# Two-layer hybrid mixer step: the 1/rms table through memory, spatial weights loaded earlier, new tokens' scores after the attention

## The chip, the cores and the metric

The kernel runs on one core of one Trainium2 chip. The metric is the device time of one launch in microseconds; before the change it is 2384.72 us, the median of three runs (2384.2 to 2386.24).

## The reference

One inference step of a two-layer decoder on 1,024 prompt tokens (width 1,024) and 8 new tokens, each with its own cache. A layer computes `h = RMSNorm(x)`, one wide projection `h @ w_in`, four branches of width 384, and a gated merge:

```
h = rms_norm(x, norm_g)
A: y = a_b * conv3(a_c * a_h)                   # short causal convolution
B: window attention, distances 0..128, 6 heads, sinks, rotary
C: y = c_u * (tril(w_spatial) @ LN(c_v) + b_spatial)   # chunks of 128 positions
D: three head pairs, windows (128,1), (512,4), (2048,16), rotary,
   weighted by their softmax denominators
out = x + (sum_n sigmoid(h @ w_merge)_n * ((y_n * silu(gate_n)) @ w_branch_n)) @ w_out
```

The new tokens run through the same layer; their attention reads keys and values of the caches instead of the prompt's. Outputs are both token groups after a final norm, and the updated caches.

## The kernel before, in words

All activations are kept channel by partition, 1,032 columns wide: 8 new tokens, then 1,024 prompt tokens. A float32 product is made of three matmuls on a high and a low half of each operand (L178, L181, L182; L372, L375, L376 for the groups whose tokens lie on the partitions). `hh` and `hl` hold the halves of `x * g` without the factor 1/rms; that factor is applied behind the products. Token-major results take it from `rtok` (one column of 128 tokens per block), channel-major ones from `rr`, a table with all 1,032 factors in every partition, and the rotation takes it through `cosT` and `sinT`, which are multiplied by `rr` once per layer.

Each weight tile is loaded by SP into `wr`, rounded by ACT into `wh` (L154), and its rest made by POOL into `wl` (L156). Weight tiles have few buffers, so the projections run in the order of the program.

Per layer the order of the program is: projections of window keys and the first window queries (`rope_products`); 1/rms (L324 to L338); the first value group `tm_v` (L408) with 9 blocks of 8 x 3 matmuls, one block of tokens after another; more window queries; the chunk branch's values `tm_group` with their statistics; the second value group; the spatial branch (L441 to L484); window attention `attend` (L632); gates; and three dilated groups, `branch_d(0..2)`. For each dilated group the new tokens' scores `decD.scores` (L651 to L668) come before the group's attention, `attention()`. They transpose the queries (L656), write them to memory and read them back into every partition (L659, L661), multiply them by the cached keys on POOL (L662), sum on DVE (L663), and take the new token's own key in a small matmul (L667). After the third group come a projection, `decode_finish` (L680 to L719: softmax over the cached keys on 8 partitions, transposed back at L713), then the weights of the three groups (`al` to `at`, L919 to L945, with the transpose at L934), the loads of the chunk branch's result `y` from memory (L952), the values of the new tokens (`values`, L731 and L733, put between the chunks of the last two gate projections), and the merge (L1000 to L1011), whose first operand `yh`, `yl` is made from `y` (L979, L980).

1/rms, before: the mean square per token is taken to `rtok`, then 9 diagonal matrices `dg` are made on DVE (L332), and a matmul with a matrix of ones (L333) puts each block's factors into all partitions.

Tiles carry a tag; the tiles of one tag share a fixed number of buffers: `ms` (small PSUM results) and `acc` (projections) three each, `dec` (caches, values, spatial weights, `y`) three, `slot` 34. Within a tag a new tile takes a buffer that an earlier one has given back.

The program's order is not the order on the engines: the framework plans all five engines with simulated times and issues what is ready by its plan, with the program's order as priority. Each engine then runs its own list in order. Inside `attend` a few groups of matmuls are pinned to the program's order (L531). `load(dst, src, dist)` ties an SP load to the projection that is `dist` marks back, and so sets how far ahead it may be issued.

Of the kernel before, what the change touches and what calls it, by code (L numbers as in the profile page):

```python
# [7 lines left out]
F32 = mybir.dt.float32  # L8
F32R = mybir.dt.float32r
AF = mybir.ActivationFunctionType  # L10
ALU = mybir.AluOpType
AX = mybir.AxisListType

P = 128
# [3 lines left out]
NS = 8  # L18
T = SEQ + NS
CH = 344  # L20
NCH = 3
MIX = 384
# [10 lines left out]
def kernel(ctx: ExitStack, tc: tile.TileContext, i, o, c):  # L33
    nc = tc.nc
    pe, act, dve, pool, sp = nc.tensor, nc.scalar, nc.vector, nc.gpsimd, nc.sync
# [5 lines left out]
    sm = ctx.enter_context(tc.tile_pool(name="sm", bufs=1))  # L41
# [13 lines left out]
    def dec(shape, name):  # L55
        return sl.tile(shape, F32, tag="dec", name=name, bufs=3)
# [7 lines left out]
    def pmisc():  # L64
        return psM.tile([P, 512], F32, tag="ms", name="ms")
# [4 lines left out]
    def dscr(name, shape):  # L70
        return dr.tile(shape, F32, tag=name, name=name)
# [20 lines left out]
    def load(dst, src, dist):  # L92
        d_ = sp.dma_start(dst, src)
        if len(marks) >= dist:
            tc.add_manual_dep(d_.ins, marks[-dist].name, nosync, reason="prefetch distance")


    ident = cp.tile([P, P], F32, name="ident")
# [3 lines left out]
    onesm = cp.tile([P, P], F32, name="onesm")  # L102
# [21 lines left out]
    for l in range(2):  # L124
# [5 lines left out]
        for b in range(NS):  # L130
# [5 lines left out]
            n = 2047 * 256 // 8  # L136
# [30 lines left out]
    def w_pair(l, c0, j):  # L167
        r = split_w([P, KT, P], [
            (lambda t: t[:, :, 0:64], win_cols(l, c0 + 64 * j, 64)),
            (lambda t: t[:, :, 64:128], win_cols(l, c0 + 192 + 64 * j, 64))])  # L170
        copy_piece()
        return r
# [78 lines left out]
    for n0, n1 in GROUPS:  # L251
        off = NS if n0 == 0 else 0
        cs = slice(NS + n0 * P - off, NS + n1 * P)
        w = cs.stop - cs.start
        for k in range(KT):
            ks_ = slice(k * P, (k + 1) * P)
            ps = pmisc() if k % 2 else pacc()
# [12 lines left out]
    for n in range(9):  # L270
        src, M = (xin[n], P) if n < 8 else (xs, NS)
        act.activation(junk[:M, :DM], src[:M, :DM], AF.Square, accum_out=sq0[:M, n:n + 1])

    for l in range(2):
# [31 lines left out]
        def rope_tile(w, name):  # L306
            return rope(rope_products([w], [slot(name)])[0])
# [5 lines left out]
        cosT, sinT = slot("cosT"), slot("sinT")  # L313
        load(cosT, c["cos"], 2)
        load(sinT, c["sin"], 2)
        rr, rtok = slot("rr"), sm.tile([P, 9], F32, tag="rtok", name="rtok", bufs=2)
        if l == 0:
            pt_ = sq0
        else:
            pt_ = pmisc()  # L320
            for n in range(9):
                cols, M = (blkcols(n), P) if n < 8 else (slice(0, NS), NS)
                pe.matmul(pt_[:M, n:n + 1], ssq[:, cols], onesm[:, 0:1], start=True, stop=True)
        for ps_, M in ((slice(0, 8), P), (slice(8, 9), NS)):  # L324
            act.activation(rtok[:M, ps_], pt_[:M, ps_], AF.Sqrt, bias=epst[:M], scale=1.0 / DM)
            dve.reciprocal(rtok[:M, ps_], rtok[:M, ps_])
        for n0, n1 in ((8, 9), (0, 4), (4, 8)):
            ps = pmisc()
            M = NS if n0 == 8 else P
            for n in range(n0, n1):  # L330
                dg = sm.tile([P, P], F32, tag="dg", name="dg", bufs=2)
                dve.tensor_scalar(dg[:M, :M], ident[:M, :M], rtok[:M, n:n + 1], None, op0=ALU.mult)  # L332
                pe.matmul(ps[:, (n - n0) * P:(n - n0) * P + M], onesm[:M], dg[:M, :M], start=True, stop=True)  # L333
            cs = slice(0, NS) if n0 == 8 else slice(NS + n0 * P, NS + n1 * P)
            w = cs.stop - cs.start
            act.activation(rr[:, cs], ps[:, :w], AF.Copy)
            dve.tensor_tensor(cosT[:, cs], cosT[:, cs], rr[:, cs], op=ALU.mult)
            pool.tensor_tensor(sinT[:, cs], sinT[:, cs], rr[:, cs], op=ALU.mult)  # L338
        cw = sm.tile([P, 3, 3], F32, tag="cw", name="cw")
        for t in range(3):  # L340
            load(cw[:, :, t], i["conv_w"][l, t].rearrange("(j p) -> p j", p=P), 2)
# [5 lines left out]
        bview = i["b_spatial"][l].rearrange("(j h) t -> h j t", h=2)  # L347
# [35 lines left out]
        def tm_v(srcs, off):  # L383

            vn = [sl.tile([P, 4, 256], F32, tag="slot", name=f"vn{off}{q}") for q in range(2)]

            def vdst(n):
                return vn[n // 4][:, n % 4] if n < 8 else vsam[:, off:off + 256]

            def ev(n, M, ps):  # L390
                act.activation(vdst(n), ps, AF.Identity, scale=rtok[:M, n:n + 1])
                if n < 8:
                    act.dma_start(vscr[n * P:(n + 1) * P, off:off + 256], vdst(n))
            tm_group(srcs, 4, ev)
            for nm, c0 in (("swa_p", 0), ("dil_p0", 128), ("dil_p1", 256), ("dil_p2", 384)):
                c1 = c0 - off
                if c1 not in (0, P):
                    continue
                dst = o[nm][l, 0, :, 1].rearrange("t h d -> t (h d)")
                nb = dst.shape[0] // P  # L400
                for n in range(nb):
                    act.dma_start(dst[n * P:(n + 1) * P, :], vdst(8 - nb + n)[:, c1:c1 + P])
                dst = o[nm.replace("_p", "_s")]
                dst = dst[l, :, dst.shape[2] - 1, 1].rearrange("b h d -> b (h d)")
                act.dma_start(dst, vsam[:, c0:c0 + P])

        kB, qB = rope(kq[0]), [rope(kq[1])]
        tm_v([(S_V, P), (D_V, P)], 0)  # L408
        qB.append(rope_tile(w_pair(l, S_Q, 1), "qB1"))
        cvt = [sl.tile([P, 2, MIX], F32, tag="slot", name=f"cv{q}") for q in range(4)]  # L410
        lnst = sm.tile([P, 9, 6], F32, tag="lnst", name="lnst")
# [26 lines left out]
            return t  # L438


        lngb, wsps = dec([P, T], "lngb"), dec([P, T], "wsp")  # L441
        wsp = wsps[:, 0:6 * P].rearrange("p (g s) -> p g s", g=6)
        bsps = [lngb[:, 6 * P:7 * P], lngb[:, 7 * P:8 * P], wsps[:, 6 * P:7 * P]]
        for h in range(2):
            for j in range(3):
                load(bsps[j][h * 64:(h + 1) * 64], bview[h, j].partition_broadcast(64), 2)
        load(lngb[:, 0:MIX], i["v_ln_g"][l].partition_broadcast(P), 2)
        load(lngb[:, MIX:2 * MIX], i["v_ln_b"][l].partition_broadcast(P), 2)
        for n in range(9):
            M = P if n < 8 else NS  # L450
            if n == 0:
# [5 lines left out]
            dve.tensor_tensor(v, v, lngb[:M, 0:MIX], op=ALU.mult)  # L457
            dve.tensor_tensor(v, v, lngb[:M, MIX:2 * MIX], op=ALU.add)
        store_later(2, o["chunk_v_s"][l].rearrange("b s c -> (b s) c"), cvs)
        load(wsp, i["w_spatial"][l].rearrange("g t s -> t g s"), 2)  # L460
        wsT = dec([P, 6, P], "wsT")
        for g0 in (0, 3):
            ps = pmisc()
# [6 lines left out]
        for j in range(3):  # L470
            ps = pmisc()
            pe.transpose(ps[:, :NS], cvs[:, j * P:(j + 1) * P], ident[:NS, :NS])
            dve.tensor_scalar(yC[j][:, 0:NS], ps[:, :NS], ws0[:, j:j + 1], bsps[j][:, 0:1], op0=ALU.mult, op1=ALU.add)
            for n0 in (0, 4):
                ps = pmisc()
                for n in range(4):
                    for h in range(2):
                        g = 2 * j + h
# [120 lines left out]
        for j in range(4):  # L599
            t = sm.tile([P, NS], F32, tag=f"qbs{j}", name=f"qbs{j}")  # L600
# [286 lines left out]
        decD = Decode("D")  # L887
        rows, attention = branch_d(0, ends)
        conv_a(0, rows)
        decD.scores(0, dqs[0], dks[0])  # L890
        attention()
        conv_a(1)
        in_a(0)
        decB = Decode("B")
# [8 lines left out]
        rows, attention = branch_d(1)  # L903
        in_a(1)
        rows()
        decD.scores(1, dqs[1], dks[1])
        attention()
        out_a(1)
        conv_a(2)
        rows, attention = branch_d(2)  # L910
        sg0 = gate_d(0)
        rows()
        decD.scores(2, dqs[2], dks[2])
        attention()
        in_a(2)
        values_d = decD.finish(OD)

# [15 lines left out]
        ps = pmisc()  # L933
# [39 lines left out]
        for bi, n in enumerate(order):  # L973
            yh, yl = [], []
            yy = ynext
            for j in range(3):
                t = yy[j]
# [5 lines left out]
            for m in range(KT):  # L983
# [14 lines left out]
                for ch in range(NCH):  # L998
                    cs = slice(ch * CH, (ch + 1) * CH)
# [4 lines left out]
                    t = ctmp("th")  # L1004
# [66 lines left out]
        for m in range(KT - NTAIL):  # L1071
            w = wout(m)
# [4 lines left out]
        for n0, n1 in GROUPS:  # L1077
            c0 = NS + n0 * P if n0 else 0
            cs = slice(c0, NS + n1 * P)
# [66 lines left out]
```

## Time and profile before

| | |
|---|---|
| median of three runs | 2384.72 us |
| the profiled execution | 2387.34 us, span 2385.6 us |
| TensorE (PE) busy | 2365.5 us, 99%; weight loads (PEld) 97% |
| DVE, POOL, ACT busy | 38%, 35%, 29% |
| chain that ended last | PE 98% |
| matmuls of L178, L181, L182 | 27% of the chain each |
| granted TensorE clock, mean | 0.991 |
| DMA | 235.82 MB, mean 99 GB/s |

A page describes one profiled execution. Busy time is the time in which an engine had an instruction running; a wait is put down to what ended last before the waiting instruction began. The clock is the share of full speed that TensorE was granted in a stretch. In the timelines `PE` is a matmul, `PEld` its weight load, `SPq` and `ACTq` the issuing of DMAs; the bracket at the end of a row is the idle time of the engine before it, and what ended it.

### The profile page before, as it was taken

Reading aid. Unit: us, or ns where it says so; the run is one execution under the profiler, and the core shown is the slowest. Engines: PE = TensorE matmul, PEld = TensorE weight load, DVE = VectorE, ACT = ScalarE, POOL = GpSimd, SP = SyncE. Lnnn points to the kernel's source line nnn. Section 1 sums busy time; section 2 is a strip of 40 time slices with the busy share of each in tenths; the row PEclk is TensorE's granted clock in tenths of the full one; section 3 lists DMA queues with packets and bytes.
Section 4 is the critical chain, followed back from the end, with each engine's and each line's share of the span. In section 5 each row is a group of like instructions: output and inputs, shape, how many; then the busy total and the mean of one; then the engine's idle time right before and its main releaser. Section 6 shows DMA issues by size and latency. Waiting matters only on the chain.

```text
span 2385.6 us, 38754 instructions
## 1 busy us (share of the span) xinstructions
PE 2365.5 (99%) x15896; PEld 2305.1 (97%) x15896; DVE 895.2 (38%) x1938; ACT 687.4 (29%) x1522; POOL 843.5 (35%) x556
## 2 busy tenths in 40 slices
PE   7999999999999999999999999999999999999999
PEld 6999999999999999999999999999999999999999
DVE  4345466335312222324333455554452221213143
ACT  5133432223212222223322244323231221212243
POOL 3333234432223444434442322353322233444330
PEclk9999999999899999999999999999989999999999
DMA  7342423433322212224542423244442122222232
GB/s 237 98 123 79 119 69 109 132 102 106 100 71 88 77 55 97 64 70 123 150 146 72 145 72 98 69 151 113 111 126 67 58 91 66 98 67 62 75 99 101
DMA packets 295962, 235.82 MB, mean 99 GB/s; under 512 B 52756, under 2 KB 279696, under 8 KB 293416
## 3 DMA queue, kind: packets, MB, share of 16 engines
q1 hardware_dynamic: 267952, 206.25, 28.8%
q10 hardware_dynamic: 27832, 27.10, 4.1%
q8 instruction: 124, 2.03, 0.4%
q14 instruction: 54, 0.44, 0.1%
HBM read 192.35 MB, written 76.47 MB: 113 GB/s over the span
## 4 chain that ended last, share of the span: by engine, by line
PE 98%; DVE 1%; DMA 0%; ACT 0%; SPq 0%; issue 0%; ACTq 0%; DVEq 0%
PE acc L181 27%; PE acc L182 27%; PE acc L178 27%; PE acc L372 2%; PE acc L375 2%; PE acc L376 2%; PE sc L540 2%; PE ms L569 2%; PE ms L558 1%; PE ms L733 1%; PE ms L479 0%; PE ms L1042 0%; DMA wr<-in_w_in_dram 0%; DVE xT L264 0%; DVE h0l L209 0%; PE ms L333 0%
## 5 line engine op out<-in xcount | busy, mean ns | idle before, releaser
L156 POOL TENSOR_TENSOR wl<-wr,wh 128x384 fp32r<-128x384 f32 (+2 forms) x228 | 476.9, 2093 | 827.3 <-ACT wh L154 698.7
L181 PE MATMUL acc<-h1l,wh 128*128 128x344 f32 x1584 | 511.5, 323 | 0.0
L182 PE MATMUL acc<-h0h,wl 128*128 128x344 f32 x1584 | 510.4, 323 | 0.0
L178 PE MATMUL acc<-h0h,wh 128*128 128x344 f32 x1584 | 509.3, 322 | 0.9 <-DVE xT L264 0.9
L178 PE MATMUL acc<-h1h,wh 128*128 128x344 f32 x1584 | 510.2, 322 | 0.0
L182 PE MATMUL acc<-h1h,wl 128*128 128x344 f32 x1584 | 509.5, 322 | 0.0
L181 PE MATMUL acc<-h0l,wh 128*128 128x344 f32 x1584 | 508.9, 321 | 0.0
L154 ACT ACTIVATE wh<-wr 128x384 fp32r<-128x384 f32 (+2 forms) x228 | 205.2, 901 | 421.4 <-PE acc L181 393.6
L1005 DVE TENSOR_TENSOR th<-acc,rr 128x344 f32<-128x344 f32 x192 | 99.1, 516 | 553.5 <-PE acc L182 553.5
L181 PEld LDWEIGHTS acc<-h1l,wh 128*128 128x128 f32 x1584 | 299.9, 189 | 4.2 <-issue 3.6
L181 PEld LDWEIGHTS acc<-h0l,wh 128*128 128x128 f32 x1584 | 299.2, 189 | 3.9 <-issue 3.5
L182 PEld LDWEIGHTS acc<-h1h,wl 128*128 128x128 f32 x1584 | 299.7, 189 | 2.8 <-issue 2.3
L178 PEld LDWEIGHTS acc<-h0h,wh 128*128 128x128 f32 x1584 | 299.1, 189 | 2.8 <-issue 1.2
L182 PEld LDWEIGHTS acc<-h0h,wl 128*128 128x128 f32 x1584 | 298.6, 189 | 2.9 <-issue 2.3
L178 PEld LDWEIGHTS acc<-h1h,wh 128*128 128x128 f32 x1584 | 299.6, 189 | 1.4 <-issue 1.0
L1011 POOL TENSOR_TENSOR mg<-mg,th 128x344 f32<-128x344 f32 x144 | 134.0, 931 | 303.3 <-DVE th L1010 303.3
L1006 ACT ACTIVATE th<-th 128x344 f32<-128x344 f32 x192 | 94.3, 491 | 496.9 <-DVE th L1005 496.4
L178 PE MATMUL acc<-yh,wh 128*128 128x344 f32 x576 | 184.4, 321 | 0.0
L182 PE MATMUL acc<-yh,wl 128*128 128x344 f32 x576 | 184.3, 320 | 0.0
L181 PE MATMUL acc<-yl,wh 128*128 128x344 f32 x576 | 184.1, 320 | 0.0
L181 PE MATMUL acc<-ml,wh 128*128 128x344 f32 (+3 forms) x384 | 123.2, 321 | 0.0
L182 PE MATMUL acc<-mh,wl 128*128 128x344 f32 (+3 forms) x384 | 123.0, 321 | 0.0
(278 smaller groups left out, 3256.6 us busy)
## 6 DMA issues: line engine op xcount, KB each, us to landing
wr<-in_w_merge_dram SPq DMA_DIRECT2D x64, 512.0 KB
out_dram<-in_cache_dil_kv_dram SPq DMA_DIRECT2D x128, 255.9 KB
wr<-in_w_in_dram SPq DMA_DIRECT2D x60, 512.0 KB
y<-yscr SPq DMA_DIRECT2D x18, 516.0 KB
wr<-in_w_branch_dram SPq DMA_DIRECT2D x48, 192.0 KB
wr<-in_w_in_dram SPq DMA_DIRECT2D x32, 256.0 KB
wr<-in_w_out_dram SPq DMA_DIRECT2D x16, 512.0 KB
out_dram<-in_cache_dil_kv_dram SPq DMA_DIRECT2D x16, 511.0 KB
```

Of the source, the lines that this page charges most:

```text
L154: act.activation(hi, raw, AF.Copy)
L156: pool.tensor_tensor(lo, raw, hi.bitcast(F32), op=ALU.subtract)
L178: mm = pe.matmul(ps[:, :n], hi[:, k], xh[k][:, cs], start=(k == 0), stop=False)
L181: pe.matmul(ps[:, :n], hi[:, k], xl[k][:, cs], start=False, stop=False)
L182: pe.matmul(ps[:, :n], lo[:, k], xh[k][:, cs], start=False, stop=(k == kt - 1))
L372: mm = pe.matmul(ps[:M, :N], lh, hi[:, k % kk], start=(k == 0), stop=False)
L375: pe.matmul(ps[:M, :N], ll, hi[:, k % kk], start=False, stop=False)
L376: pe.matmul(ps[:M, :N], lh, lo[:, k % kk], start=False, stop=(k == KT - 1))
L540: pin(pe.matmul(ps[:, h, a * 256:a * 256 + u.nk], u.qs[h], u.ks[h], start=True, stop=True))
L1005: dve.tensor_tensor(t, pg[:, :CH], rr[:, cs], op=ALU.mult)
L1006: act.activation(t, t, AF.Tanh, scale=0.5)
L1011: pool.tensor_tensor(mg[m][:, cs], mg[m][:, cs], t, op=ALU.add)
```

## The change

Three edits. 1/rms: `rtok` is written to a scratch in memory by two ACT stores, in token order, and read back by one SP load that repeats it in all 128 partitions; `cosT` and `sinT` are multiplied over their full width. Spatial weights: the loads of `lngb`, `bsps` and `wsp` move from behind the second value group to behind the first, ahead of the second window query projection. New tokens' scores: in all three dilated groups `decD.scores` moves behind `attention()`.

```diff
--- before.py
+++ after.py
@@ -324,18 +324,13 @@
         for ps_, M in ((slice(0, 8), P), (slice(8, 9), NS)):
             act.activation(rtok[:M, ps_], pt_[:M, ps_], AF.Sqrt, bias=epst[:M], scale=1.0 / DM)
             dve.reciprocal(rtok[:M, ps_], rtok[:M, ps_])
-        for n0, n1 in ((8, 9), (0, 4), (4, 8)):
-            ps = pmisc()
-            M = NS if n0 == 8 else P
-            for n in range(n0, n1):
-                dg = sm.tile([P, P], F32, tag="dg", name="dg", bufs=2)
-                dve.tensor_scalar(dg[:M, :M], ident[:M, :M], rtok[:M, n:n + 1], None, op0=ALU.mult)
-                pe.matmul(ps[:, (n - n0) * P:(n - n0) * P + M], onesm[:M], dg[:M, :M], start=True, stop=True)
-            cs = slice(0, NS) if n0 == 8 else slice(NS + n0 * P, NS + n1 * P)
-            w = cs.stop - cs.start
-            act.activation(rr[:, cs], ps[:, :w], AF.Copy)
-            dve.tensor_tensor(cosT[:, cs], cosT[:, cs], rr[:, cs], op=ALU.mult)
-            pool.tensor_tensor(sinT[:, cs], sinT[:, cs], rr[:, cs], op=ALU.mult)
+
+        rscr = dscr(f"rscr{l}", [T])
+        act.dma_start(rscr[0:NS], rtok[:NS, 8])
+        act.dma_start(rscr[NS:T].rearrange("(n i) -> i n", i=P), rtok[:, 0:8])
+        sp.dma_start(rr, rscr.partition_broadcast(P))
+        dve.tensor_tensor(cosT, cosT, rr, op=ALU.mult)
+        pool.tensor_tensor(sinT, sinT, rr, op=ALU.mult)
         cw = sm.tile([P, 3, 3], F32, tag="cw", name="cw")
         for t in range(3):
             load(cw[:, :, t], i["conv_w"][l, t].rearrange("(j p) -> p j", p=P), 2)
@@ -406,6 +401,15 @@
 
         kB, qB = rope(kq[0]), [rope(kq[1])]
         tm_v([(S_V, P), (D_V, P)], 0)
+        lngb, wsps = dec([P, T], "lngb"), dec([P, T], "wsp")
+        wsp = wsps[:, 0:6 * P].rearrange("p (g s) -> p g s", g=6)
+        bsps = [lngb[:, 6 * P:7 * P], lngb[:, 7 * P:8 * P], wsps[:, 6 * P:7 * P]]
+        for h in range(2):
+            for j in range(3):
+                load(bsps[j][h * 64:(h + 1) * 64], bview[h, j].partition_broadcast(64), 2)
+        load(lngb[:, 0:MIX], i["v_ln_g"][l].partition_broadcast(P), 2)
+        load(lngb[:, MIX:2 * MIX], i["v_ln_b"][l].partition_broadcast(P), 2)
+        load(wsp, i["w_spatial"][l].rearrange("g t s -> t g s"), 2)
         qB.append(rope_tile(w_pair(l, S_Q, 1), "qB1"))
         cvt = [sl.tile([P, 2, MIX], F32, tag="slot", name=f"cv{q}") for q in range(4)]
         lnst = sm.tile([P, 9, 6], F32, tag="lnst", name="lnst")
@@ -438,14 +442,6 @@
             return t
 
 
-        lngb, wsps = dec([P, T], "lngb"), dec([P, T], "wsp")
-        wsp = wsps[:, 0:6 * P].rearrange("p (g s) -> p g s", g=6)
-        bsps = [lngb[:, 6 * P:7 * P], lngb[:, 7 * P:8 * P], wsps[:, 6 * P:7 * P]]
-        for h in range(2):
-            for j in range(3):
-                load(bsps[j][h * 64:(h + 1) * 64], bview[h, j].partition_broadcast(64), 2)
-        load(lngb[:, 0:MIX], i["v_ln_g"][l].partition_broadcast(P), 2)
-        load(lngb[:, MIX:2 * MIX], i["v_ln_b"][l].partition_broadcast(P), 2)
         for n in range(9):
             M = P if n < 8 else NS
             if n == 0:
@@ -457,7 +453,6 @@
             dve.tensor_tensor(v, v, lngb[:M, 0:MIX], op=ALU.mult)
             dve.tensor_tensor(v, v, lngb[:M, MIX:2 * MIX], op=ALU.add)
         store_later(2, o["chunk_v_s"][l].rearrange("b s c -> (b s) c"), cvs)
-        load(wsp, i["w_spatial"][l].rearrange("g t s -> t g s"), 2)
         wsT = dec([P, 6, P], "wsT")
         for g0 in (0, 3):
             ps = pmisc()
@@ -887,8 +882,8 @@
         decD = Decode("D")
         rows, attention = branch_d(0, ends)
         conv_a(0, rows)
+        attention()
         decD.scores(0, dqs[0], dks[0])
-        attention()
         conv_a(1)
         in_a(0)
         decB = Decode("B")
@@ -903,15 +898,15 @@
         rows, attention = branch_d(1)
         in_a(1)
         rows()
+        attention()
         decD.scores(1, dqs[1], dks[1])
-        attention()
         out_a(1)
         conv_a(2)
         rows, attention = branch_d(2)
         sg0 = gate_d(0)
         rows()
+        attention()
         decD.scores(2, dqs[2], dks[2])
-        attention()
         in_a(2)
         values_d = decD.finish(OD)
```

## Rows read from the trace of the kernel before

**Rows 1.** Part 1 of the page: engine, busy us, share of the span, instructions.

```profile
PE 2365.5 (99%) x15896; PEld 2305.1 (97%) x15896; DVE 895.2 (38%) x1938; ACT 687.4 (29%) x1522; POOL 843.5 (35%) x556
```

**Rows 2.** Waits of TensorE: line, releaser, us in total, times, longest.

```profile
PE ms L333 <- DVE dg L332: 3.8, 3, 1.5
```

**Rows 3.** Timeline of TensorE, layer 0, first value group: start us, us, line, tiles, form.

```profile
50.42 0.28 PE L372 MATMUL acc<-wh,h0h 128*128 128x256 f32 x1
...
71.77 0.28 PE L372 MATMUL acc<-wh,h0h 128*128 128x256 f32 x1
...
79.92 0.28 PE L372 MATMUL acc<-wh,h0h 128*8 128x256 f32 x1
...
82.67 0.32 PE L178 MATMUL acc<-h0h,wh 128*128 128x344 f32 x1
```

**Rows 4.** Windows: stretch, length, busy us of PE, PEld, DVE, ACT, POOL, clock, DMA.

```profile
52.10:55.60 3.50, 0.66 (x5) 0.49 (x4) 3.49 (x4) 0.62 (x3) 3.34 (x3) 1.00 0.25 60
55.60:60.30 4.70, 4.70 (x28) 4.70 (x28) 0.57 (x2) 0.00 (x0) 0.00 (x0) 0.64 0.99 263
```

**Rows 5.** Timeline of TensorE, layer 1, first value group.

```profile
1222.38 0.38 PE L372 MATMUL acc<-wh,h1h 128*128 128x256 f32 x1
...
1251.61 0.32 PE L178 MATMUL acc<-h1h,wh 128*128 128x344 f32 x1
```

**Rows 6.** Tile `wl`, 38 to 62 us: ns min/median/max, first and last start.

```profile
L156 POOL TENSOR_TENSOR wl<-wr,wh x3: 1798/2364/2417, 41.1 to 53.4; 128x1024 fp32r<-128x1024 f32 x2, 128x768 fp32r<-128x768 f32 x1
```

**Rows 7.** Timeline of SP and of ACT, first 12 us.

```profile
2.15 0.41 SPq L242 DMA_DIRECT2D gcol<-in_norm_g_dram  x1
...
6.32 1.28 ACT L207 ACT_TABLE_LOAD   x1 [6.32 <-DMA gcol<-in_norm_g_dram]
```

**Rows 8.** Chain that ended last: start us, us, line, count.

```profile
131.87 0.65 PE sc L540 x8
```

**Rows 9.** Timeline of DVE, layer 0, spatial branch.

```profile
159.85 3.84 DVE L457 TENSOR_TENSOR cv<-cv,lngb 128x384 f32<-128x384 f32 x8 [3.44 <-DMA lngb<-in_v_ln_g_dram]
```

**Rows 10.** Timeline of TensorE, layer 0, third dilated attention and its end.

```profile
542.98 0.27 PE L656 MATMUL ms<-ident,dqs 128*8 128x128 f32 x1
...
579.79 0.66 PE L569 MATMUL ms<-pt,v 128*64 128x128 f32 x8
580.38 0.82 PE L680 MATMUL ms<-ident,sd 128*8 128x128 f32 x6
...
592.64 0.53 PE L713 MATMUL ms<-ident,sx 8*128 8x8 f32 x6
593.10 0.29 PE L934 MATMUL ms<-ident,ew 128*48 128x128 f32 x1
...
596.88 1.09 PE L733 MATMUL ms<-pd,cD 128*64 128x1 f32 x16
```

**Rows 11.** Timeline of DVE, same stretch.

```profile
554.54 1.22 DVE L663 TENSOR_REDUCE sd<-qb 128x16 f32<-128x1024 f32 x1 [5.38 <-POOL qb L662]
...
582.34 0.21 DVE L932 TENSOR_TENSOR ew<-ew,mx 128x48 f32<-128x48 f32 x1
...
589.27 0.95 DVE L709 TENSOR_TENSOR sx<-sx,dw 8x774 f32<-8x774 f32 x1
...
613.54 3.03 DVE L980 TENSOR_TENSOR yl<-y,yh 128x1032 fp32r<-128x1032 f32 x1 [0.60 <-ACT yh L979]
```

**Rows 12.** Timeline of SP's queue, same stretch.

```profile
595.17 4.04 SPq L944 DMA_DIRECT2D at<-ascr  x6
...
607.42 0.32 SPq L93 DMA_DIRECT2D y<-yscr  x1
```

**Rows 13.** Windows, end of the third dilated attention, both layers.

```profile
580.40:616.60 36.20, 36.20 (x258) 35.30 (x257) 23.88 (x45) 8.89 (x15) 8.18 (x4) 0.81 0.54 138
1751.50:1787.00 35.50, 35.50 (x254) 34.60 (x253) 23.06 (x44) 8.79 (x15) 8.97 (x4) 0.81 0.56 142
```

**Rows 14.** Timeline of POOL, layer 0, window branch's gate.

```profile
422.66 3.88 POOL L748 TENSOR_TENSOR OB<-OB,th 128x344 f32<-128x344 f32 x4 [7.02 <-DVE OB L736]
```

## The prediction

> **What bounds the kernel now.** The first thing to read is part 1 of the page: TensorE is busy for 99% of the span, every other engine for less than 40% [rows 1]. So another engine's work or a DMA counts only where it leaves TensorE idle, slows its clock or adds instructions to it. The list of waits of TensorE shows how little is left to win: the one wait that the change touches is that of L333 for `dg`, 3.8 us over both layers [rows 2]. The next view is the timeline of TensorE at the two places where its stream is disturbed, and the windows around them with the granted clock; these are the start of each layer, where the edit to 1/rms stands, and the end of the third dilated attention, where the moved scores stand.
>
> The profiled execution took 2387.34 us around its span of 2385.6; the median of the runs shown is 2384.72. I work out a difference against the profiled execution and apply it to the median.
>
> **Part 1, 1/rms through memory: what goes.** Each layer loses 9 small matmuls (18 instructions of L333), 9 DVE products `dg`, three ACT copies and their waits. The worth is read from the value group that they cut into, from its first matmul to the first matmul behind it. In layer 0 that is 50.42 to 82.67, 32.25 us [rows 3]. Undisturbed, such matmuls start every (79.92 - 71.77) / 69 = 0.118 us (69 of them start between those two rows), and the group has 9 blocks x 8 x 3 = 216, so 25.5 us. The disturbance costs 6.7 us. It includes an idle stretch of 2.84 us (52.10 to 55.60, 0.66 busy) and 4.7 us at a granted clock of 0.64 behind it, which is (1 - 0.64) x 4.7 = 1.7 us [rows 4]. In layer 1 the group takes 1251.61 - 1222.38 = 29.23 us [rows 5], so the disturbance costs 3.7 us. The most that can be won is 10.4 us.
>
> What is late next in layer 0 is the second half of the group's weights: `wl` of that half is not ready before about 53.4, when POOL begins its next one [rows 6]. TensorE stopped at 52.1, so 1.3 us of the idle stretch stay; whether the clock falls for them as it did for 2.84 us is open (0 to 1.7 us). Bounds 10.4 - 1.3 - 1.7 = 7.4 and 10.4; I take 8.5, nearer the lower end because the weights are a row and not a guess.
>
> **Part 1: what comes.** Two small ACT stores with 1,032 four-byte elements, one SP load that waits for them and copies 4 KB to 128 partitions, one DVE and one POOL product of 1,032 columns instead of three of each. No row has that store. The nearest is the load of `gcol`, 2,048 four-byte elements: issued at 2.15, and ACT stood until 6.32 for it, 4.2 us [rows 7]. The broadcast is of the shape of `qb`, whose round trip is in the 12.8 us below. TensorE's wait for `dg`, which needs the same 1/rms, begins at 52.1, so the table is in SBUF by about 52 + 4.2 + 12.8 = 69 at the latest, and its first user on TensorE, the first scores, runs at 131.87 [rows 8]. Hidden, 0; if all of the cover were gone it would be those 17 us. Behind the load on SP stand weight loads that are issued far ahead; behind the products on DVE and POOL stands only the rotation that needs them.
>
> **Part 2, spatial weights earlier.** Nine loads, none new, move ahead of two projection groups. What waits today is DVE, 3.44 us for `lngb` [rows 9]; TensorE has no row of waiting for them. The window attention can begin sooner since its value tile takes a buffer that the spatial work holds, but a stage whose TensorE is full gains nothing from an earlier start. I take 0; bounds -1 and +1, SP's extra issues against DVE's wait.
>
> **Part 3, new tokens' scores behind the attention.** This is the part that can cost. The PSUM tiles `ms` have three buffers, and the trace shows them handed out in program order: `sd` is complete at 555.76 (L663), but its transposes (L680) start at 580.38, right behind the last result matmul (L569, 579.79); `ew` is ready at 582.55 (L932), but its transpose (L934) starts at 593.10, right behind L713 [rows 10, 11]. So in the changed program the transpose of the query (L656), today at 542.98 and inside the attention, starts where L680 starts now. From L656 to the end of L663 is 555.76 - 542.98 = 12.8 us, a round trip through two DMAs, POOL and DVE; L680 moves back by that. From L680 to L713 are 12.3 us now; 2.4 of them are TensorE coming late (L709 ends at 590.22) and some 1.4 are the `al` chain ahead on DVE, both of which the longer wait absorbs: about 8.5 are left. L713 comes at 580.4 + 12.8 + 8.5 = 601.7 instead of 592.64, 9 us later; I take off 0.5 for an attention without the scores in its way.
>
> Does the merge wait for that? L934 (in order behind L713) feeds `ewt`, `ascr`, the `at` loads and, on the same SP queue behind them, the loads of `y` [rows 12]; the last of these also needs the buffer that the last value matmul frees. The split of the last `y` (L980) ends at 616.57 [rows 11], and the merge cannot go past its first product before. From the attention's end to there is 36.2 us, and the windows show TensorE full all along, at a clock of 0.81 (0.81 in layer 1 too) [rows 13]: 36.2 x 0.81 = 29.3 us of work at full clock. So there is nothing in hand: work and chain end together today, and a chain that is 8.5 us longer is idle time, less what the last `y` catches up. Bounds per layer 3 and 12.8; I take 7, two layers 14. The other two moved scores are not on such a chain; those of the first group delay the window branch's, where POOL already stands 7.02 us [rows 14] without any idle time of TensorE, so 0, at worst 3.
>
> What the clock adds is the last question. The rows show it falling behind idle time (0.64) and also inside the full stretch above, whose one-column value matmuls are slow. The Trainium skill, "TensorE: Matmul & The Clock Gate" (Part 1, on the clock gate), says that the gate follows how busy the array has been, and that idle gaps between bursts put it back to half rate. By that rule each new gap before the merge costs another 1.7 us as in [rows 4], and the sum would be 3.4 us higher. The rows agree behind the 2.84 us gap.
>
> **Sum.** -8.5 + 0 + 14 = +5.5 us: 2390.2 for the median, 2392.8 for a profiled execution like the one shown.
>
> **Rivals.** *Covered* (faster): the scores of the third group find a place earlier, or gate tiles fill TensorE until the merge, and each layer loses 1 us or less. It decides at whether L656 runs before the last L569. For it: POOL, DVE and SP have room during the attention. Against it: the order rows above. -8.5 + 2 = -6.5, 2378. *Half covered*: the chain's shift is 4 us, since plan and execution already differ by the 2.4 us seen at L713; -8.5 + 7 = -1.5, 2383. *Chain in full*: 12.8 us per layer, DVE standing for `qb` while gate products wait behind it as it stood 5.38 us at L663; -7.4 + 25.6 = +18, 2403. *The stall stays*: the idle time at 52 was the weights' all along, and part 1 wins only instructions; of layer 0's 6.7 us stay 6.7 - 2.84 - 1.7 = 2.2, and -2.2 - 3.7 + 14 = +8, 2393.
>
> **Numbers.** The sum's own case 0.50 (2386 to 2396), covered 0.22, half covered 0.13, chain in full 0.07, stall stays 0.08. A measurement of this kernel can't tell less than 0.2%, 4.8 us, from no change: below 2379.9 lie nearly all of covered and a little of half covered, 0.24; above 2389.5 lie 0.28 of the sum's case, chain in full and stall stays, 0.43; between them 0.33. The range 2377 to 2398 leaves out part of covered and chain in full.
>
> **What would show it.** Part 1: no row of L333, the first value group about 27 us in layer 0 and 25.5 in layer 1, `cosT` and `sinT` products once per layer and no wait of TensorE before the first scores. Part 2: L457 without a wait for `lngb`, the second pair of scores earlier than today. Part 3: L656 of the third group right behind the last L569 in both layers, L663 about 13 us later, then idle time of TensorE with a lower clock ahead of the first `yh` products. I am wrong if that stretch is no longer than 36 us, or if TensorE has a new wait elsewhere, for `rr`, `cosT` or a gate's buffer.

## The result, and the profile after

The changed kernel takes 2422.63 us (median of 4; 2416.93 to 2425.22) against 2384.46 us before (median of 4, one run more than above): a ratio of 1.0158, with an interval of 1.0137 to 1.0179. The forecast was 2390.2, range 2377 to 2398. The profiled execution took 2425.22 us, its span is 2423.5, 37.9 us more than the span before.

Cutting both spans at the same matmuls shows where the 37.9 us are. The cuts are the first value matmul of a layer, the first L178 matmul behind that group, the last result matmul of the third dilated attention, the last `yh` matmul of the merge, and the last matmul; all are starts of rows in the timeline of TensorE, where like matmuls in a row are one row. Times in us:

| stage | before | after | difference |
|---|---|---|---|
| start to the first value matmul | 50.42 | 52.45 | +2.0 |
| layer 0, first value group | 32.25 | 34.10 | +1.9 |
| layer 0, on to the end of the third attention | 497.12 | 498.59 | +1.5 |
| layer 0, on to the last `yh` matmul | 527.14 | 536.78 | +9.6 |
| on to layer 1's first value matmul | 115.45 | 115.42 | 0.0 |
| layer 1, first value group | 29.23 | 41.05 | +11.8 |
| layer 1, middle | 499.27 | 500.87 | +1.6 |
| layer 1, last stage | 527.00 | 536.60 | +9.6 |
| on to the last matmul | 102.63 | 102.55 | -0.1 |

So there are two places, and each is in both layers: the first value group (+13.7 together, where 8.5 were to be won) and the stage behind the third attention (+19.2, where 14 were to be lost).

TensorE in part 1 of the page after, busy time and share, beside [rows 1]:

```profile
PE 2374.6 (98%) x15860; PEld 2312.9 (95%) x15860; DVE 896.8 (37%) x1916; ACT 685.9 (28%) x1516; POOL 855.5 (35%) x552
```

The waits of TensorE after (line, releaser, us in total, times, longest), where [rows 2] had `dg`:

```profile
PE acc L367 <- ACT vn L386: 13.1, 2, 6.9
PE ms L708 <- DVE sx L704: 8.7, 2, 4.4
PE acc L178 <- ACT vn L386: 6.5, 1, 6.5
PE acc L178 <- ACT yh L974: 4.8, 2, 2.6
```

L333's wait is gone and four others have come. L367 is the first matmul of a value block (L372 before) and L386 the ACT instruction that evicts such a block; three accumulators are in the ring, so when three evictions are missing TensorE stands. Why ACT was late is read from the chain of waits in layer 0 after (start, us, what):

```profile
52.25 7.29 DMA rscr<-rtok
...
59.69 0.33 SPq L331
...
60.12 6.04 DMA wr<-in_w_in_dram
...
66.18 0.52 ACTq L290
...
66.74 0.48 ACT vn L386
...
67.27 0.58 PE acc L367
```

and from the timeline of ACT (ACTq is its queue of DMA issues), same stretch:

```profile
50.84 0.38 ACTq L330 DMA_DIRECT2D rscr<-rtok  x1
...
52.25 0.53 ACTq L329 DMA_DIRECT2D rscr<-rtok  x1
...
53.04 0.61 ACTq L290 DMA_DIRECT2D qs<-kB  x1
...
53.69 6.20 ACTq L290 DMA_DIRECT2D qs<-kB  x3
59.99 6.71 ACTq L290 DMA_DIRECT2D qs<-qB  x4
66.74 0.84 ACT L386 ACTIVATE vn<-acc,rtok 128x256 f32<-128x256 f32 x2 [12.64 <-DMA wr<-in_w_in_dram]
```

L290 are the eight copies that rotate the first key and query tile. They have nothing to do with 1/rms. In the timeline of ACT before, they went out one behind the other, in 54.10 to 59.33:

```profile
54.10 2.54 ACTq L290 DMA_DIRECT2D qs<-kB  x4
56.73 2.60 ACTq L290 DMA_DIRECT2D qs<-qB  x4
```

Here they take from 53.04 to 66.70, and the evictions are behind them in ACT's order. They stop three times. The fourth goes out at 59.38, as the stores of 1/rms land: the first row of the chain is the second of the two, 8 elements, issued 1.4 us behind the one of 1,024, and it lands at 59.54. The sixth goes out at 64.54, beside the first user of the table, DVE's product L332 at 64.61, which waited for the load. The eighth goes out at 66.18, when a weight load lands that it does not read (60.12 + 6.04 = 66.16). The instruction list of the changed program shows the link: every DMA reports on one of eight semaphores in turn, and an issue also waits until the DMA that had its semaphore before has landed.

```
SP  L93  DMA wr_941<-in_w_in_dram 128x2x384 [waits DMAHW7_49,Pool_49]
ACT L290 DMA qs_553<-qB0_359 32x1032        [waits DMAHW7_49]
```

Both also report on the semaphore that they wait for, so the copy waits for the weights. That weight load stands on SP behind the load of 1/rms (L331), which waits for the store. So store, load, weights, copy and eviction form one chain, and TensorE's end of it costs twice, as the windows show (stretch, length, busy us of PE, PEld, DVE, ACT, POOL, granted clock, DMA share, GB/s):

```profile
61.00:67.00 6.00, 0.14 (x2) 0.00 (x0) 2.36 (x2) 0.26 (x1) 2.33 (x1) 0.88 0.99 274
67.00:72.00 5.00, 4.73 (x22) 4.73 (x23) 4.65 (x2) 1.06 (x3) 4.92 (x3) 0.50 0.54 152
```

6 us idle, and then 5 us at a granted clock of 0.50, the lower of its two levels (1.2 GHz). In layer 1 the chain of waits passes twice through ACT:

```profile
1238.45 7.82 DMA rscr<-rtok
1246.33 4.92 DMA rr<-rscr
1251.27 0.52 ACTq L290
...
1252.48 0.94 ACT vn L386 x3
...
1258.34 19.08 DMA vscr<-vn
1277.49 0.33 ACTq L388
1277.87 0.48 ACT vn L386
1278.39 0.66 PE acc L178
```

Here a copy goes out at 1251.27, 0.02 us after the load of 1/rms has landed. Then a store of `vn`, issued at 1258.34, lands 19.08 us later; the store that is next on its semaphore holds up ACT until 1277.49, and TensorE waits 6.5 us more.

The other place, the end of the third attention in layer 0, in the timeline of TensorE after (beside [rows 10]; L651, L675, L708 and L929 are L656, L680, L713 and L934 of before):

```profile
585.14 0.66 PE L564 MATMUL ms<-pt,v 128*64 128x128 f32 x8
585.73 0.27 PE L651 MATMUL ms<-ident,dqs 128*8 128x128 f32 x1
...
597.68 0.38 PE L675 MATMUL ms<-ident,sd 128*8 128x128 f32 x2
...
608.59 0.80 PE L708 MATMUL ms<-ident,sx 8*128 8x8 f32 x6 [4.39 <-DVE sx L704]
609.33 0.41 PE L929 MATMUL ms<-ident,ew 128*48 128x128 f32 x1
...
624.49 0.65 PE L178 MATMUL acc<-yh,wh 128*128 128x344 f32 x1 [2.16 <-ACT yh L974]
```

and in the windows, beside [rows 13], where the whole stretch had no idle time and a clock of 0.81:

```profile
585.00:608.50 23.50, 19.20 (x129) 18.20 (x127) 16.26 (x38) 6.20 (x13) 6.47 (x6) 0.99 0.51 155
608.50:624.50 16.00, 13.75 (x116) 13.20 (x116) 4.75 (x11) 1.06 (x1) 0.00 (x0) 0.50 0.79 184
624.50:632.00 7.50, 7.50 (x35) 7.50 (x36) 5.03 (x4) 2.13 (x2) 4.85 (x2) 0.72 0.19 70
```

The query transpose comes right behind the last result matmul, and L708 22.9 us after that transpose; before, L713 came 12.3 us after L680, which stood in its place. TensorE runs out of work for 4.39 us ahead of L708 and for 2.16 us ahead of the first `yh` products, together 6.6 of the 9.6 us. Some 2 more are the clock: busy time x (1 - clock) is 13.75 x 0.50 + 7.5 x 0.28 = 9.0 us here and 36.2 x 0.19 = 6.9 us in [rows 13]; before, too, the clock stood at 0.50 from 600 to 610, among the one-column value matmuls. Part 2 did what it says: DVE's first product with `lngb` runs without a wait (3.44 us in [rows 9]), and its stage is no shorter for it (+1.5):

```profile
144.63 0.55 DVE L453 TENSOR_TENSOR cv<-cv,lngb 128x384 f32<-128x384 f32 x1
```

### The profile page after: what moved, and what is told of

Read it like the earlier page. It is cut to its first block, busy times and chain, and to the rows that moved or that the text cites. A ratio compares the mean times of both kernels' runs of the same rounds, so it can differ in the third digit from the quotient of the medians.

```text
span 2423.5 us, 38651 instructions
## 1 busy us (share of the span) xinstructions
PE 2374.6 (98%) x15860; PEld 2312.9 (95%) x15860; DVE 896.8 (37%) x1916; ACT 685.9 (28%) x1516; POOL 855.5 (35%) x552
## 4 chain that ended last, share of the span: by engine, by line
PE 91%; DMA 4%; DVE 2%; ACT 1%; SPq 1%; issue 0%; POOL 0%; ACTq 0%; DVEq 0%; POOLq 0%
PE acc L178 26%; PE acc L182 26%; PE acc L181 26%; PE acc L367 2%; PE acc L371 2%; PE acc L370 2%; PE sc L535 2%; PE ms L564 2%; PE ms L553 1%; DMA vscr<-vn 1%; DMA rscr<-rtok 1%; DMA y<-yscr 1%; DMA wr<-in_w_in_dram 1%; DVE h0l L209 1%; PE ms L474 0%
## 5 line engine op out<-in xcount | busy, mean ns | idle before, releaser
L156 POOL TENSOR_TENSOR wl<-wr,wh 128x384 fp32r<-128x384 f32 (+2 forms) x228 | 482.8, 2119 | 826.4 <-ACT wh L154 725.3
L178 PE MATMUL acc<-h1h,wh 128*128 128x344 f32 x1584 | 512.0, 323 | 6.5 <-ACT vn L386 6.5
L178 PE MATMUL acc<-h0h,wh 128*128 128x344 f32 x1584 | 511.1, 323 | 0.9 <-DVE xT L264 0.9
L178 PEld LDWEIGHTS acc<-h1h,wh 128*128 128x128 f32 x1584 | 300.0, 189 | 11.9 <-ACT vn L386 6.8
L178 PEld LDWEIGHTS acc<-h0h,wh 128*128 128x128 f32 x1584 | 299.4, 189 | 6.2 <-issue 4.2
L1001 ACT ACTIVATE th<-th 128x344 f32<-128x344 f32 x192 | 94.3, 491 | 497.1 <-DVE th L1000 493.7
L178 PE MATMUL acc<-yh,wh 128*128 128x344 f32 x576 | 184.8, 321 | 4.8 <-ACT yh L974 4.8
## 6 DMA issues: line engine op xcount, KB each, us to landing
out_dram<-in_cache_dil_kv_dram SPq DMA_DIRECT2D x16, 511.0 KB
```

The source lines that it names most:

```text
L156: pool.tensor_tensor(lo, raw, hi.bitcast(F32), op=ALU.subtract)
L178: mm = pe.matmul(ps[:, :n], hi[:, k], xh[k][:, cs], start=(k == 0), stop=False)
L1001: act.activation(t, t, AF.Tanh, scale=0.5)
```

## The experiments

Ratios are against runs of the kernel before on the same chip, with their 95% intervals; the stages are those of the table above, from the profiled execution of each kernel, in us.

| kernel | median | ratio | value group L0, L1 | middle L0, L1 | last stage L0, L1 |
|---|---|---|---|---|---|
| before | | | 32.3, 29.2 | 497.1, 499.3 | 527.1, 527.0 |
| after | 2422.6 | 1.0158 | 34.1, 41.1 | 498.6, 500.9 | 536.8, 536.6 |
| e1 part 1 | 2409.5 | 1.0108 (1.0092 to 1.0125) | 34.5, 40.1 | 505.7, 506.6 | 525.7, 525.5 |
| e2 part 2 | 2389.6 | 1.0014 (1.0005 to 1.0023) | 29.4, 29.1 | 499.9, 503.0 | 527.0, 524.9 |
| e3 part 3 | 2407.8 | 1.0098 (1.0084 to 1.0112) | 32.3, 29.2 | 499.0, 497.8 | 538.1, 536.2 |
| e4 part 3, other tile | 2396.6 | 1.0055 (1.0041 to 1.0069) | 29.3, 29.3 | 505.0, 503.8 | 526.1, 525.7 |
| e5 copies behind | 2391.4 | 1.0016 (1.0005 to 1.0028) | 25.5, 25.6 | 497.4, 514.4 | 525.8, 525.3 |
| e6 load behind too | 2388.0 | 1.0000 (0.9986 to 1.0014) | 25.5, 25.5 | 498.2, 511.0 | 525.5, 527.1 |
| e7 store by rows | 2401.3 | 1.0061 (1.0043 to 1.0079) | 32.3, 33.6 | 502.0, 505.7 | 525.8, 527.1 |
| e8 part 3, two groups | 2385.9 | 0.9996 (0.9986 to 1.0006) | 29.3, 29.2 | 497.2, 498.7 | 525.8, 525.5 |
| e9 e6 and e8 | 2386.7 | 1.0001 (0.9988 to 1.0013) | 25.5, 25.5 | 497.2, 505.3 | 527.0, 525.3 |
| e10 copies further behind | 2391.8 | 1.0028 (1.0014 to 1.0041) | 25.5, 27.2 | 499.6, 508.1 | 525.4, 525.9 |
| e11 change, both mended | 2391.5 | 1.0024 (1.0013 to 1.0036) | 25.5, 25.6 | 498.0, 511.0 | 527.0, 528.1 |
| e12 part 1, layer 0, mended | 2378.2 | 0.9969 (0.9957 to 0.9981) | 25.5, 29.2 | 498.6, 497.1 | 525.8, 525.5 |

**Each part alone.** e1, e2 and e3 are the kernel before with one part of the change each.

> The kernel before with part 1 alone (1/rms through memory). Theory A (the evictions of the first value group stand behind the rotation's copies on ACT, which wait for the new store and load): a wait of TensorE of 6 to 7 us inside the first value group of each layer, for ACT's evictions; the group takes about 34 us in layer 0 and 36 to 41 in layer 1; 2388 to 2398. Rival B (the nine spatial loads of part 2 crowd the DMA engines and part 1 does what I forecast): no such wait, groups of 27 and 26 us, about 2377.

> The kernel before with part 2 alone (nine spatial loads earlier). Theory A: within 3 us of before, 2382 to 2388, value groups as before (32 and 29 us). Rival B: a wait of TensorE for the evictions of the first value group, at the least that of 6.5 us at the end of layer 1's group, so 2391 to 2400.

> The kernel before with part 3 alone (all three groups' scores behind the attention). Theory C (the third group's query transpose takes its PSUM tile behind the last result matmul, and the finish chain starts 12 us later): idle time of TensorE behind the third attention, 7 to 10 us per layer, 2398 to 2405. Rival D (in the changed kernel the late layer start shifted loads into this stretch and cost half of it): 2390 to 2396.

e1 has the value groups of the changed kernel without part 2, so theory A holds and rival B falls. It costs 24 us, though, more than expected; waits of TensorE in e1:

```profile
PE acc L367 <- ACT vn L386: 18.6, 2, 11.8
PE ms L651 <- DVE dqs L816: 7.8, 2, 4.0
```

The second row is in the middle stage: the query transpose ahead of the second attention waits for a query tile whose rotation has become late. In layer 0, 2.2 of these us are the last copy of that tile on DVE: L816 takes 2.31 us from 466.76, beside a POOL product that ends with it, and took 0.16 before. The whole change does not have this wait, since part 3 puts that transpose behind the attention. This is the greater part of why the parts alone (24, 4 and 22 us by the medians) add up to more than the 38 of the whole. The hold in layer 1 ends in another way than in the whole change: a copy goes out at 1247.80, 0.02 us after the load of 1/rms has landed, and then the issue of the last copy alone takes 5.08 us; the store of `vn` that adds 6.5 us in the whole change holds up nothing here. Why that issue was slow is open.

e2 costs 0.14%, more than the nothing that I took, and its 2389.6 lies between the ranges of A and B; but its value groups are 29.4 and 29.1, and the one wait for an eviction behind them is 1.9 us, so B falls. e3 has the last stages of the changed kernel and costs somewhat more than expected, so C holds and D falls.

**The tile of the query transpose.** e4 is e3 with one word changed in the scores:

```
-                ps = pmisc()
+                ps = pacc()
                 pe.transpose(ps[:NS, :P], q, ident)
```

> Part 3 alone, but the query transpose takes its PSUM tile from the accumulators' ring instead of that of the attention's small tiles. Theory C: the transpose runs inside the attention again, no new idle time behind it, 2381 to 2389. Rival D' (the scores are late for another reason: the cache tile, POOL or the broadcast): the idle time stays, 2396 to 2405.

The transpose (L656 here) is inside the attention again, which ends at 586.21, and the last stage is as before; timeline of TensorE in e4:

```profile
546.90 0.27 PE L656 MATMUL acc<-ident,dqs 128*8 128x128 f32 x1
```

So the order in which the `ms` tiles are handed out made the third group late, and D' falls for that stage. The median, 2396.6, is where D' and not C had put it: the kernel is still 0.55% slower, and all of that is in the middle stages (+7.9 and +4.5), with new waits, the first of them ahead of the first dilated attention; that the borrowed `acc` tiles cause them is not shown:

```profile
PE sc L540 <- DVE dq L298: 4.8, 2, 2.4
...
PE ms L558 <- DVE s L627: 2.8, 2, 1.4
```

**Which order held the evictions.** e5 and e6 are part 1 alone with lines moved behind the first value group, `tm_v`: in e5 the rotation (and so the copies), in e6 the load with its products as well.

In e5:

```
-        kB, qB = rope(kq[0]), [rope(kq[1])]
         tm_v([(S_V, P), (D_V, P)], 0)
+        kB, qB = rope(kq[0]), [rope(kq[1])]
```

In e6:

```
-        sp.dma_start(rr, rscr.partition_broadcast(P))
-        dve.tensor_tensor(cosT, cosT, rr, op=ALU.mult)
-        pool.tensor_tensor(sinT, sinT, rr, op=ALU.mult)
...
-        kB, qB = rope(kq[0]), [rope(kq[1])]
         tm_v([(S_V, P), (D_V, P)], 0)
+        sp.dma_start(rr, rscr.partition_broadcast(P))
+        dve.tensor_tensor(cosT, cosT, rr, op=ALU.mult)
+        pool.tensor_tensor(sinT, sinT, rr, op=ALU.mult)
+        kB, qB = rope(kq[0]), [rope(kq[1])]
```

> Part 1 alone, with the rotation of the first key and query tiles (and so its eight copies on ACT) put behind the first value group; the load of 1/rms stays where part 1 has it on SP, ahead of weight loads. Theory A (the evictions stood behind the copies): no wait of TensorE for evictions, value groups 25.5 to 28 us in both layers, 2375 to 2384. Rival E (the load on SP holds back weights that the value group or the next group needs): a wait for weights or evictions stays, groups over 31 us, 2388 or more.

> As the one before, and the load of 1/rms with its two products put behind the weight loads of the value group as well. Theory A: the same as there within 3 us, 2375 to 2384, since SP's order was harmless by itself. Rival E: only here does the gain of part 1 come, 2375 to 2382, and 8 us or more below the one before. If the rotation is now late for the first scores, TensorE waits before them and the middle stage is longer.

Both value groups fall to 25.5 us, the 216 x 0.118 of the prediction, and in e5 the load is still ahead of the weights on SP. So it was the copies on ACT, and rival E falls for this stage. In layer 0 of e5, timeline of ACT, the copies now go out without a long hold behind evictions that run:

```profile
58.50 0.47 ACT L386 ACTIVATE vn<-acc,rtok 128x256 f32<-128x256 f32 x1 [2.40 <-PE acc L371]
...
81.67 3.30 ACTq L290 DMA_DIRECT2D qs<-qB  x4
```

The totals missed the expectation all the same: layer 1 gives 12 to 15 us back in its middle stage. Waits of TensorE in e5: the first at the transpose that e1 had shown, the second for the second query tile's evictions, which now stand behind the copies.

```profile
PE ms L651 <- DVE dqs L816: 4.8, 1, 4.8
...
PE acc L367 <- ACT qB L281: 3.3, 1, 3.3
```

**The store.** e7 is part 1 in its own order, with 1/rms turned by TensorE ahead of the store:

```
+        pe.transpose(pr[:8, 0:P], rtok[:, 0:8], ident)
+        dve.tensor_copy(rT[:, 0:P], pr[:8, 0:P])
+        act.dma_start(rscr[NS:T].rearrange("(n i) -> n i", i=P), rT[:, 0:P])
-        act.dma_start(rscr[NS:T].rearrange("(n i) -> i n", i=P), rtok[:, 0:8])
```

> Part 1 alone in its own order, but 1/rms is turned by TensorE first, so that the store has 8 rows of 512 bytes and one of 32 instead of 1,032 elements of 4 bytes. Theory A1 (the store is slow because of its many small pieces): it lands in 2 to 4 us instead of 7.3 to 7.8, the copies start by so much earlier, and the waits of TensorE for evictions shrink to 0 to 3 us in layer 0: 2382 to 2395. Rival A2 (7 us are the latency of any store under this load): landing and waits as with part 1 alone, 2405 to 2413.

The chain of waits in e7, layer 0:

```profile
54.67 2.87 DMA rscr<-rT
...
57.59 7.71 DMA rr<-rscr
...
65.33 0.52 ACTq L290
...
65.89 0.48 ACT vn L392
```

A1 is right on the store: both have landed 2.87 us after the first issue, where the two of the changed kernel took 8.7 (50.84 to 59.54). On the wait it is half wrong: TensorE still waits 9.6 us over both layers for evictions (18.6 in e1), and 2401.3 lies between both ranges. In layer 0 the load goes out 2.1 us earlier than in the changed kernel but takes 7.71 us, and the copy is held until it lands (57.59 + 7.71 = 65.30; the copy goes out at 65.33). This is the clearest row for the shared semaphores: the copy reads nothing of that load. The Trainium skill, "DMA: Bandwidth & Descriptors" ("Anatomy of one DMA"), says that DMA engines do not wait on semaphores, and that the wait is on the sequencer that issues the DMA. The rows agree: it is ACT's own order that stands still.

**Two groups of part 3, and both repairs together.** e8 moves the scores of the first two groups only, e9 does so in e6, and e10 puts load and copies of e9 one group further, behind the second query tile's products.

```
-        decD.scores(0, dqs[0], dks[0])
         attention()
+        decD.scores(0, dqs[0], dks[0])
...
-        decD.scores(1, dqs[1], dks[1])
         attention()
+        decD.scores(1, dqs[1], dks[1])
```

and for e10, beside e9:

```
         tm_v([(S_V, P), (D_V, P)], 0)
+        kq.append(rope_products([w_pair(l, S_Q, 1)], [slot("qB1")])[0])
         sp.dma_start(rr, rscr.partition_broadcast(P))
...
-        kB, qB = rope(kq[0]), [rope(kq[1])]
-        qB.append(rope_tile(w_pair(l, S_Q, 1), "qB1"))
+        kB, qB = rope(kq[0]), [rope(kq[1]), rope(kq[2])]
```

> Part 3 for the first two dilated groups alone; the third group's scores stay ahead of their attention. Theory C (only the third group's place costs): the stage from the last attention to the end of the merge as before (527 us), 2383 to 2389. Rival F (the first group's move delays the window branch's decode chain): the middle stage 5 us or more longer per layer, 2393 to 2400.

> The kernel with load and copies behind the value group, and the first two groups' scores behind their attention. Theory G (in it TensorE's second new wait, 4.5 us at the query transpose ahead of the second attention plus a lower clock, was only the scores' place): that wait is gone, layer 1's middle stage 4 to 9 us shorter, 2377 to 2383. Rival H (the second dilated query tile itself is late, and its first scores wait instead): the wait moves to the scores, 2384 to 2390.

> As the one before, with the load of 1/rms and all twelve copies of the first three tiles put one group further, behind the second query tile's products. Theory A (copies on ACT hold back whatever eviction stands behind them, so they belong where evictions have time): the two waits of layer 1 behind the value group (1.7 and 2.8 us, and the lower clock after them) go too, value groups stay 25.5 us, 2372 to 2379, faster than before. Rival I (rotation too late for the first scores, or the copies hold back the local values' evictions instead): a new wait of TensorE between 95 and 140 or 1265 and 1305, 2380 to 2392.

e8 is as before in every stage but the value group of layer 0 (29.3, see below), so moving the first two groups' scores costs nothing, as the prediction took it, and F falls. In e9 the wait at the transpose is gone and layer 1's middle is 5.6 us shorter than in e6, as G says, and no wait for the scores has come in its place; but only the profiled execution (2381.72) lies in G's range, the median of 12 runs is 2386.7, and no gain against before can be claimed. e10 missed: its waits are

```profile
PE acc L368 <- POOL wl L156: 5.1, 2, 3.1
...
PE sc L535 <- DVE qB L298: 1.7, 1, 1.7
```

so the rotation is too late for the first scores of layer 1, and POOL takes the rotation's products ahead of weights that TensorE waits for. Rival I holds, time and all (2391.8).

**The whole change, mended, and the best version.** e11 is the changed kernel with load and copies behind the first value group and the third group's scores ahead of their attention again. e12 is the kernel before with part 1 in layer 0 alone, in e6's order:

```
+        if l == 0:
+            rscr = dscr(f"rscr{l}", [T])
+            act.dma_start(rscr[0:NS], rtok[:NS, 8])
+            act.dma_start(rscr[NS:T].rearrange("(n i) -> i n", i=P), rtok[:, 0:8])
+        else:
+            for n0, n1 in ((8, 9), (0, 4), (4, 8)):
...
+        if l == 0:
+            tm_v([(S_V, P), (D_V, P)], 0)
+            sp.dma_start(rr, rscr.partition_broadcast(P))
+            dve.tensor_tensor(cosT, cosT, rr, op=ALU.mult)
+            pool.tensor_tensor(sinT, sinT, rr, op=ALU.mult)
         kB, qB = rope(kq[0]), [rope(kq[1])]
-        tm_v([(S_V, P), (D_V, P)], 0)
+        if l == 1:
+            tm_v([(S_V, P), (D_V, P)], 0)
```

> The changed kernel with its two costs taken out: load of 1/rms and the first copies put behind the first value group, and the third group's scores put back ahead of their attention; part 2 and the first two groups stay. Theory A with C: these two were nearly all of the 38 us; value groups 25.5 us, last stage 525 to 527 us in both layers, 2383 to 2393. Rival J (part 2 has a cost of its own of 10 us or more once the others are gone): 2395 or more.

> The kernel before with part 1 in layer 0 alone, its load and copies behind the value group; layer 1 as before. Theory A: layer 0's value group 25.5 us and no new wait behind it there, layer 1 untouched (29.2 and 499 us), so 3 to 6 us faster than before: 2379 to 2383. Rival K (the gain is lost again to shifted loads in layer 0's middle stage or in layer 1): 2385 to 2390.

Of the 38 us, e11 leaves 5 (0.24%), and its last stages and value groups are where A and C put them; J falls. Its middle stage of layer 1 is 11.7 us longer than before, as in e6. e12 beats both kernels: 2378.2 us, 0.31% below the kernel before and at the good end of what A gave; K falls. Part 1 of its page, beside [rows 1]:

```profile
PE 2359.0 (99%) x15878; PEld 2298.2 (97%) x15878; DVE 878.8 (37%) x1927; ACT 686.2 (29%) x1519; POOL 844.1 (36%) x554
```

## Why the prediction was wrong

**The step that failed** is in part 1, what comes: "Hidden, 0; if all of the cover were gone it would be those 17 us. Behind the load on SP stand weight loads that are issued far ahead". The prediction has the table in SBUF by about 69 at the latest, and its first product ran at 64.6; that this came out near is luck, since the stores took 8.7 us and not 4.2, and the load some 4.9 and not 12.8. TensorE waited nowhere for the table itself. But I looked only for users of the table and at one queue. The load on SP and the store on ACT are also members of a chain of DMAs over both queues, through the eight semaphores, and ACT's evictions stand behind eight copies of that chain. The 17 us are named, but they are in no bound and no rival: instead of -8.5 the value groups gave +1.9 and +11.8 (e1: +2.2 and +10.8). Of the 32 us by which the profiled execution missed the forecast these are 22; the last stages are 5, the start and the middle stages the rest. None of the rivals had this mechanism, and so the range was too low: it was not a mis-sized term but a wait that I did not look for. The signs of being wrong named new waits for `rr`, `cosT` or a gate's buffer; the one that came was for a PSUM tile.

**What goes, in part 1**, was right in place and close in size. Without the hold the groups take 25.5 us (e5, e6), so 6.8 and 3.7 us go against the profiled execution, the 10.4 named as the most. The 1.3 us that I kept for the weights of the group's second half are not there. The 6.7 us in layer 0, however, are not the same in each kernel: with the same code in that stage e3 took 32.3 us, but e2, e4 and e8 took 29.3 to 29.4, so that in those only 3.8 were to be won there.

**Part 2** was taken at 0 with bounds of 1 us; e2 measured 0.14%, some 3.3 us. In its profile the middle stages are 2.8 and 3.7 us longer and 1.9 us are a wait of TensorE for an eviction in layer 1. Nine loads more ahead in the same turn of semaphores can do that, but no run takes it apart, so the cause is open.

**Part 3** was right in its mechanism and under-sized. The transpose of the third group starts right behind the last result matmul, in both layers, as forecast; `sd` is complete 11.6 us after it (597.3 - 585.7 in the row of DVE below; 12.8 forecast); L675 to L708 takes 10.9 (8.5 forecast). The last stage is 9.6 us longer per layer, not 7: I took L680 to L713 2.4 us too short and let the last `y` catch up 1.5 us, where the shift of L708 (22.9 - 12.3 = 10.6) shows 1.0. e4 shows that the tile ring is the cause, e8 that the other two groups cost nothing.

```profile
596.09 1.22 DVE L658 TENSOR_REDUCE sd<-qb 128x16 f32<-128x1024 f32 x1 [2.81 <-POOL qb L657]
```

**The clock** fell behind each new gap, to 0.50 for 5 us behind the 6 us gap of layer 0, so 2.5 us, and cost some 2 us in the last stage of layer 0; it was a small part of what was missing. The Trainium skill, "TensorE: Matmul & The Clock Gate" (Part 1), has the rule that idle gaps put the gate back to half rate; the trace agrees with it, and the 3.4 us that the prediction named by it for the two merges and left out of its sum were of the right sign and near the measured size.

The start of the kernel, 2.0 us longer, is not the change's: kernels with the same code there took 51.2 to 52.4 (e2, e3, e4, e8).

**What stays open**: why the `vn` store of layer 1 took 19.08 us. Three cache copies were issued next to it (1258.12 to 1260.88), and from 1262.95 to 1276.5 the DMA queues moved only 64 packets, 30 of SP's with 1.30 MB and 33 of ACT's with 0.03 MB: the rest of the stores went in small pieces beside large ones. But before, the stores of `vn` also ran beside such copies (1234 to 1248, 0.91 MB of SP's and 0.79 MB of ACT's) and TensorE had no wait for evictions there, so what made it so slow here is only argued. Open too is what lengthens layer 1's middle stage in e5, e6, e9 and e11; in e11 the issue of ACT's stores behind the value group takes 10.37 us from 1243.96, and the longest wait of TensorE there, 5.1 us, is for the eviction behind them.

## What to carry to other kernels

A DMA that waits is never alone: before a transfer that waits for another is put on a queue, list what is issued behind it on that engine, what takes the same completion semaphore after it on any engine, and whose evictions or weights stand behind those. A latency that is hidden from the users of its data can still stop the engine that bounds the kernel, so bound it by the whole round trip and not at zero. Of a tile ring ask in which order the program hands its tiles out: a step moved behind a loop starts behind the loop's last tile, wherever its inputs are ready, and another ring (e4, at a price elsewhere) or the old place (e8) takes that back.

## What the runs showed of the hardware

Two stores of 1,024 and of 8 elements of 4 bytes had landed 8.7 and 8.3 us after the first issue (from 50.84 and from 1237.98); the 8 elements, issued second, took 7.29 and 7.82 us by themselves. One of 8 rows of 512 bytes and one of 32 bytes, in e7, had landed after 2.87. The broadcast of the same 4 KB to 128 partitions took 4.9 to 7.7 us (1246.33 after, 57.59 in e7). A gap of 6 us in TensorE's work was followed by 5 us at a clock of 0.50, where [rows 4] had 4.7 us at 0.64 behind 2.8 us. The eight copies L290, which went out in 5.2 us before, took 13.7 us where their semaphores were held. A DVE copy of 8 columns took 2.31 us beside a POOL product in e1, and 0.16 before.
